# A hybrid SSD and attention layer on one core: another order of issue for its middle part

## The chip, the cores and the metric

The kernel runs on one core of a Trainium2 chip. The metric is the device time of one execution in microseconds, lower is better; the kernel before is given by the median of three runs, beside the lowest and the highest. The engines of the core are TensorE (PE in the profile, with PEld for its weight loads), VectorE (DVE), ScalarE (ACT), GpSimd (POOL) and SyncE (SP, which here only issues transfers).

## The reference

One layer of a trunk with two groups of heads in parallel, Mamba-2 SSD heads and latent attention (MLA) heads, and a SwiGLU FFN, for 512 columns of a new stream (prompt) and 64 columns of a running one (sample). All in fp32.

```python
def hybrid_layer(x, ckv_past, krope_past, ssm_h0, conv_buf, p):
    h = rmsnorm(x, p['norm_mix'])
    proj = h @ p['w_in']                      # z, xbc, dt, cq, ckv
    ...
    xbc, conv_new = causal_conv(xbc, conv_buf, p['conv_w'], p['conv_b'])
    ...
    y, h_new = ssd_scan(xh, dt, A, Bm, Cm, ssm_h0)        # chunks of 64
    y = y + p['d_skip'].astype(jnp.float32)[:, None] * xh.astype(jnp.float32)
    y = y.reshape(b, T, SSD_WIDTH) * jax.nn.silu(z.astype(jnp.float32))
    y_ssd = rmsnorm(y, p['ssd_norm']).astype(x.dtype)
    ...
    o_lat = mla_attend(q_lat, q_rope, q_pos, keys_c, keys_r, jnp.arange(P + T))
    o = jnp.einsum('bthl,lhd->bthd', o_lat, p['w_uv']).reshape(b, T, MLA_WIDTH)
    x = x + jnp.concatenate([y_ssd, o], axis=-1) @ p['w_out']
    hf = rmsnorm(x, p['norm_ffn'])
    x = x + (jax.nn.silu(hf @ p['w_gate']) * (hf @ p['w_up'])) @ p['w_down']
    return x, c_kv, k_rope, h_new, conv_new
```

The model width is 1024, the FFN's 2816; 8 SSD heads and 8 attention heads of 64; the sample stream has 256 past positions. Outputs are the normed x of both groups, the new latent and rotary keys, the SSD states and the convolution's last rows.

## The kernel before

**Tiling.** The 576 columns (512 prompt and 64 sample) are cut into two halves of 288, which are the free size of the large products; features lie in tiles of 128 on the partitions. An fp32 product is made of three: weights and operand are each split into a high part (ScalarE copies it to fp32r, L120) and a low part (VectorE subtracts, L121 for weights, L154 in `split_scaled` for operands), and `product` issues high·high, high·low and low·high for each 128 of the contraction. So a tile named `wl_...` is the low part of a weight, and a product needs both.

**Stages.** 1. The first tiles of the input projection. 2. Convolution tiles (`conv_tile`, L396), with small copies of the tiles' ends to `nconv` on POOL (L405, L406). 3. The SSD scan, chunk by chunk, with the z tiles (`z_tile`, L471), the v tiles (L602) and the projections of head pairs (`pair_proj`, L618) between. The cumulated steps are transposed on TensorE, copied by VectorE to `cumT` (L386) and written to DRAM as `cumD` by POOL (L387, in `step_rows`); `chunk_a` loads rows of it back on SP as `cumb` (L496) and `ecp` (L502), POOL masks `cumb` with an affine_select (L523, `chunk_e`), and ScalarE makes the decays E of it (L529). 4. Attention by pairs of heads: `scores` (L673) into PSUM tiles `sc` (prompt blocks, two heads) and `sc_s` (sample); `soft` (L656) takes the negated maximum on VectorE (`mx`, L663), the exponential with its sum on ScalarE (`pr`, L664), the reciprocal (`sm`, L665) and the scaling (L670); `turn` and `turn_s` (L692, L706) transpose `pr` on TensorE into `ptp` and copy it to `pt`; `values` makes `pv` and `pvs`, and `cat` (L715) splits them into the operand `cat_o`: ScalarE's copies (L719), then VectorE's subtractions (L720). 5. Output projection: `cat_tile` (L771) makes the operands `cat_y` of the SSD heads (xsd L772, then the low part `a`, L154), and `out_tile` (L746) multiplies: tiles `ps_o0_t` take the SSD heads (weights `wl_out0`, `wh_out0`), tiles `ps_o1_t` the attention heads; VectorE adds each half of a tile into x (L758), which frees its PSUM bank. 6. `x_operands` (L809) makes the FFN's operands `xop` and `xop_last` (seven blocks of a Strassen-like scheme with seven products), with subtractions of `x` blocks (L824 to L827) and low parts (L831); `gu_weights` (L834) makes the combined weights (additions L840 to L843, then `split_weights`). 7. The FFN, from about 240 us to the end: gate and up products (L883), down products, the last norm and the outputs.

**PSUM.** Most tiles of stages 3 to 5 come from a pool `bank(tag, name)` (L455) with three banks under "sc", and banks under "pp" and "hm": a new tile waits until the reader of an earlier one in the same bank is done.

**Order.** All instructions are first made stage by stage. Then `issue_in_order` (L1327) chains the instructions of each engine in the order of a table `ISSUE` (L1339): a text of places among those made on that engine, which `_places` decodes ("469-634" stands for a run). Each engine then issues strictly in this order, and its instructions wait for their operands by semaphores. The table covers 4190 places on TensorE, 893 on VectorE, 688 on ScalarE, 160 on POOL and 133 on SP. SP's list is the order of the loads, each of which is issued only when the one before it could be.

```python
for name, text in ISSUE.items():
    made = [i for i in nc.cur_bb.bb.instructions if i.engine == engines[name].engine]
    order = list(_places(text))
    for a, b in zip(order, order[1:]):
        tc.add_manual_dep(made[b], made[a].name, info, reason="issue order")
```

Of the kernel before, what the change touches and what calls it, by code (L numbers as in the profile page):

```python
# [1326 lines left out]
def issue_in_order(tc, nc):  # L1327
# [15 lines left out]
154-169 174-175 170-171 270-274 176-221 172-173 222-269 275-370 373-420 371 421-468 372 469-634 637 641-644 638-640  # L1343
657-660 635-636 665-726 737-758 661-664 763 645-652 759-760 727-736 764-766 653-656 767-818 859 761-762 819-826 860-864
833-840 827-832 865-870 841-852 871-874 853-856 875-880 857-858 881-887 904-912 888 892-899 889-891 900-903 925-926
913-921 927-934 922-924 935 939-940 936-938 949-957 964-966 941 945-948 967-968 958-963 969 942-944 970-975 987 976-979
1003 980-986 991-993 988 1004-1005 1015-1021 1006-1014 1022-1024 994-996 1025-1026 1029-1034 1043-1045 997-998 989
1000-1002 999 1046-1054 990 1035-1039 1059-1061 1040-1042 1062-1064 1027-1028 1075-1077 1081-1092 1055-1057 1078-1080
1093-1096 1058 1097-1104 1121-1123 1071-1072 1124-1129 1065 1068-1070 1073 1105-1107 1066-1067 1074 1130-1156 1119-1120
1229-1240 1157 1108-1114 1158 1241-1245 1253-1262 1246-1247 1115-1118 1159-1161 1176-1177 1248-1252 1263-1264 1162-1175  # L1350
1265 1180 1178 1181-1183 1179 1266-1268 1277-1279 1184-1187 1190-1195 1269-1276 1196-1204 1188-1189 1205-1223 1227-1228
1224-1226 1280-1297 1301-1303 1298-1300 1304-1321 1342-1343 1348-1355 1344-1347 1322-1341 1356-1511 1572 1512-1559
1575-1576 1560-1571 1577 1596-1598 1578 1573-1574 1593 1584-1585 1579 1581-1583 1602-1604 1623-1625 1594-1595 1614 1586
1605-1606 1590-1592 1611-1613 1632-1634 1587-1589 1608-1610 1607 1580 1599-1601 1620-1622 1641 1626-1628 1647-1649
# [10 lines left out]
81 57 65 56 89 66 83 90 130 91 95 84 96-97 46 98-100 113-114 103 115 47 139 116 93 117 92 111 118 122-123 148 124  # L1365
101-102 125 120 126-127 119 131-133 155 134 129 135-136 140-142 149 104 152 128 150 153 170 143-144 138 145 147 151 154
156 137 146 174 157 178 159 171-172 187 169 160 158 161-162 176 203 163 175 183 180 164 167 165-166 168 211 181 177 188
173 189 182 184 190-191 179 192-194 185-186 220 195 204-206 196-202 207 282 208 212-214 209 216 218 215 210 221 217 219
222-225 228 226-227 229-230 239 249 240 231 288 250 241 233 242 251 253 252 254 234 232 258 235 255 236 257 256 301 261
237 259 238 260 243 262 264 245 263 247 244 268 246 248 269-270 283 265 284 271-273 289 280 274 276 275 281 266 291 311  # L1370
285 277 312 267 292 296 293 310 294 278-279 313 297 300 286-287 290 303 306 298 320 299 304 302 307 321 356 305 322 316
295 317 308 357 324 318 314 323 309 330 315 319 358 327 361 331 325-326 359 334 332 328-329 335 338 343 333 344 339 336
340 346 345 337 349 352 360 341 353 351 342 354 350 347 355 362 371 348 364-365 363 366 369-370 367-368 376 384 372 378
377 379-380 373 383 381 374 391 382 375 387 399 389 385 390 388 386 394 393 395 392 397 396 414 400 398 402 401 403 406
404 411 408 405 407 412 456 410 415 417 413 458 419 416 418 409 427 425 420 426 423 422 421 432 424 428 463 457 430 429
431 433 436 435 437 460 434 438 445 459 440 461-462 446-447 439 441 449 448 442 467 469 450 471 470 468 451 466 464 472
452-453 443-444 473 454 475 474 455 465 476 485 481 477 490-491 478 482 492-493 483 494-496 479-480 497 504 484 509-512
516 486 498 513 500 514 501 515 502 526-529 533 540 487-489 530 541-543 499 505-506 503 517 531 523-524 518-519 507-508
525 532 534 522 544 535 560 520 536 521 545 537 539 546 538 561-562 547-548 563 549 568 564 550-553 555 569-570 554 559
571 556 572-575 565 576-577 566 557 584-585 578 586 579-580 558 592 567 593-594 587-588 581-582 595 583 597 596 589  # L1380
598-601 590 604 591 602-603 614-617 605 621 606 618 607-608 619-620 613 628-630 622 631 611 632 612 623 610 609 624 635
633 625 634 627 626 648-650 636 651 637 656 652 638-641 643 657-658 642 647 659 644 660-663 653 664-665 654 645 672-673
666 674 667-668 646 680 655 681-682 675-676 669-670 683 671 685 684 677 686-689 678 692 679 690-691 702-705 693 709 694
706 695-696 707-708 701 716-718 710 719 699 720 700 711 698 697 712 723 721 713 722 715 714 736-738 724 739 725 744 740
726-729 731 745-746 730 735 747 732 748-751 741 752-753 742 733 760-761 754 762 755-756 734 768 743 769-770 763-764
757-758 771 759 773 772 765 774-777 766 780 767 778-779 790-793 781 797 782 794 783-784 795-796 789 804-806 798 807 787
808 788 799 786 785 800 811 809 801 810 803 802 824-826 812 827 813 833 828 814-817 819 834-835 818 823 836 820 837-840
829 841-842 830 821 849-850 843 851 844-845 822 858 831 859-860 852 832 853 846-847 861 848 863 862 854 864-867 855 870
856 868 874 869 875-877 881 878 857 879 871 880 873 872 882-892
# [3 lines left out]
64 44 46-48 53-54 68 55 57-58 72 59 61-62 76 63 65-67 77 69-71 73 92 74-75 94 79 88 78 81 104 82 90 84 116 86-87 103 85  # L1393
83 100 98 80 97 89 99 102 101 96 91 126 105 93 111 109-110 156 115 95 107-108 113 122 114 112 142 117 163 106 118-119
136 127 137 134 128 140 135 124 121 120 139 129 138 141 130 123 143 131 125 150 146 149 132 210 133 145 148 154 152 151
# [127 lines left out]
```

## Time and profile before

| | before |
|---|---|
| median of 3 runs | 629.37 us (628.84 to 630.38) |
| the profiled execution's own time | 629.94 us |
| its span in the profile | 628.2 us |
| granted clock, mean | 0.997 |
| TensorE, VectorE, ScalarE, POOL busy | 99%, 86%, 64%, 19% of the span |
| DMA | 89.19 MB, mean 142 GB/s |

A row of a timeline gives the start, the duration, the engine, the line of the kernel, and the operation as output <- inputs, where the engine's idle time ahead of it and what ended it stand in brackets. Matmuls are pipelined: one of 288 columns shows some 0.29 us, though the next starts 0.13 us later. A chain of waits is read from the end backwards: each piece is what released the next. The number of instructions in a row (x3) follows the tiles' names, which stand without their buffer numbers.

### The profile page before, as it was taken

How to read it: one execution, taken by the hardware profiler on the slowest of the kernel's cores; microseconds unless marked ns; L12 is line 12 of the kernel's file. 1: busy time of each engine (PE TensorE's matmuls, PEld its weight loads, DVE VectorE, ACT ScalarE, POOL GpSimd, SP SyncE). 2: the span in 40 equal slices, each digit the busy share in tenths (PEclk: the TensorE clock that was granted, in tenths of full speed). 3: DMA queues.
4: the chain of work that ended last, by engine and by line, in shares of the span. 5: the costliest groups of instructions: out<-in, count | busy, mean ns of one | idle time of the engine just before them, and what ended most of it. 6: DMA issues, size and time to landing. Idle time of an engine off the chain costs nothing.

```text
span 628.2 us, 12100 instructions
## 1 busy us (share of the span) xinstructions
PE 618.9 (99%) x4639; PEld 592.2 (94%) x4639; DVE 539.6 (86%) x941; ACT 399.6 (64%) x767; POOL 117.1 (19%) x169
## 2 busy tenths in 40 slices
PE   9999999999999999999999999999999999999996
PEld 8899999986788799999999999999999999999996
DVE  6999986889876699999999888988899789986556
ACT  7655445779775577766566676666757664767364
POOL 1322104231010000001300330033104220313322
PEclk9999999999999999999999999999999999999998
DMA  8322374322241123235633986398737893589924
GB/s 318 139 62 73 93 197 130 116 75 76 79 141 39 59 111 105 84 122 182 246 142 106 202 185 150 98 186 192 181 101 154 200 213 100 97 217 261 251 46 150
DMA packets 39593, 89.19 MB, mean 142 GB/s; under 512 B 4570, under 2 KB 14312, under 8 KB 39280
## 3 DMA queue, kind: packets, MB, share of 16 engines
q1 hardware_dynamic: 26416, 63.12, 30.5%
q0 software_dynamic: 12400, 24.73, 21.3%
q8 instruction: 36, 0.59, 0.4%
q10 hardware_dynamic: 720, 0.57, 0.3%
q14 instruction: 21, 0.17, 0.1%
HBM read 62.74 MB, written 24.53 MB: 139 GB/s over the span
## 4 chain that ended last, share of the span: by engine, by line
PE 89%; DVE 7%; issue 1%; ACT 1%; DMA 1%; POOL 0%; POOLq 0%; DVEq 0%; ACTq 0%
PE ps_x L883 21%; PE ps_d L1073 14%; PE ps_z L883 10%; PE ps_in L289 7%; PE ps_y L883 5%; PE ps_z L466 4%; PE ps_o L466 4%; PE ps_first L138 3%; PE ps_l L289 3%; PE ps_d L289 2%; PE sc L680 2%; PE ps_p L883 2%; PE pv L727 1%; PE ptp L702 1%; PE ps_q L466 1%
## 5 line engine op out<-in xcount | busy, mean ns | idle before, releaser
L883 PE MATMUL ps_x<-xop,wh_gu_S 128*128 128x288 f32 x378 | 75.9, 292 | 0.0
L121 DVE TENSOR_TENSOR wl_gu_S<-gu,wh_gu_S 128x1024 fp32r<-128x1024 f32 x44 | 53.3, 1220 | 8.3 <-ACT wh_gu_S L120 6.0
L883 PEld LDWEIGHTS ps_x<-xop,wh_gu_S 128*128 128x128 f32 x378 | 60.1, 188 | 0.2 <-ACT u L986 0.2
L1087 POOL DMA_DIRECT2D acc<-fz x32 | 27.9, 906 | 164.3 <-ACT fz L1084 135.7
L120 ACT CAST wh_gu_S<-gu 128x1024 fp32r<-128x1024 f32 x44 | 46.3, 1052 | 15.3 <-PE ps_y L883 7.8
L883 PE MATMUL ps_x<-xop,wl_gu_S 128*128 128x288 f32 x189 | 55.1, 291 | 0.0
L883 PEld LDWEIGHTS ps_x<-xop,wl_gu_S 128*128 128x128 f32 x189 | 35.4, 188 | 0.0
L120 ACT CAST wh_gu_A<-gu 128x1024 fp32r<-128x1024 f32 x22 | 23.1, 1049 | 10.4 <-PE ps_x L883 7.1
L883 PE MATMUL ps_z<-xop,gu_a 128*128 128x288 f32 x189 | 29.3, 291 | 0.0
L466 PE MATMUL ps_o<-a,wh_out 128*128 128x288 f32 x128 | 28.6, 308 | 0.4 <-DVE a L154 0.3
L121 DVE TENSOR_TENSOR wl_gu_A<-gu,wh_gu_A 128x1024 fp32r<-128x1024 f32 x22 | 26.8, 1220 | 1.2 <-ACT wh_gu_A L120 0.7
L1032 POOL DMA_DIRECT2D acc<-dn x8 | 4.4, 544 | 120.3 <-ACT dn L1031 120.3
L289 PE MATMUL ps_in<-a,wh_in 128*128 128x288 f32 x128 | 26.1, 296 | 0.5 <-DVE sp_a L369 0.5
L883 PE MATMUL ps_x<-xop_last,wh_gu_S 128*128 128x288 f32 x126 | 26.5, 291 | 0.0
L883 PEld LDWEIGHTS ps_z<-xop,gu_a 128*128 128x128 f32 x189 | 26.3, 187 | 0.0
L1073 PE MATMUL ps_d<-pair,d_1h 128*128 128x288 f32 x128 | 26.1, 292 | 0.0
L883 PE MATMUL ps_z<-xop,wh_gu_S 128*128 128x288 f32 x126 | 25.8, 293 | 0.0
L289 PE MATMUL ps_in<-xs,wh_in 128*128 128x288 f32 x128 | 25.7, 293 | 0.0
L466 PE MATMUL ps_o<-cat_o,wh_out 128*128 128x288 f32 x128 | 25.4, 293 | 0.2 <-DVE x L758 0.2
L883 PE MATMUL ps_x<-xop,wh_gu_A 128*128 128x288 f32 x126 | 25.5, 293 | 0.0
L883 PE MATMUL ps_y<-xop,wh_gu_A 128*128 128x288 f32 x126 | 25.5, 293 | 0.0
L289 PE MATMUL ps_l<-pr,wh_dl 128*128 128x320 f32 (+1 forms) x128 | 25.4, 294 | 0.0
(434 smaller groups left out, 2216.7 us busy)
## 6 DMA issues: line engine op xcount, KB each, us to landing
gu<-in_w_gu SPq DMA_DIRECT2D x44, 512.0 KB, 5.3
wr_d<-in_w_down SPq DMA_DIRECT2D x18, 512.0 KB, 3.8
acc<-fz POOLq DMA_DIRECT2D x16, 288.0 KB, 7.1
acc<-da POOLq DMA_DIRECT2D x16, 288.0 KB, 8.0
acc<-dc POOLq DMA_DIRECT2D x16, 288.0 KB, 8.6
wr_in<-in_w_in SPq DMA_DIRECT2D x8, 512.0 KB, 3.8
wr_out<-in_w_out SPq DMA_DIRECT2D x8, 512.0 KB, 3.3
cumb<-cumD SPq DMA_DIRECT2D x5, 512.0 KB, 4.5
```

Of the source, the lines that this page charges most:

```text
L120: act.copy(hi, raw)
L121: dve.tensor_tensor(lo, raw, hi.bitcast(F32), ALU.subtract)
L138: pe.matmul(ps[:m, hf, : cols.stop - cols.start], w, x[:, cols], start=start and k == 0 and i == 0, stop=stop and k == last and i == 2,)
L289: pe.matmul(ps, w, x[:, cols], start=first and k == 0 and i == 0, stop=last and k == len(terms) - 1 and i == 2,)
L466: pe.matmul(ps[:, :n], w, x[:, cols], start=k == 0 and i == 0, stop=k == len(terms) - 1 and i == 2,)
L680: pe.matmul(s[:, :nk], qs[:, j, q0 : q0 + P], ks[:, j, :nk], start=True, stop=True)
L702: pe.transpose(pp[:, k : k + P], prs[p, i][:, j, b * P : b * P + P], ident)
L727: pe.matmul(pv[64 * j : 64 * j + 64, b * P :], V[b][:, h * HD : (h + 1) * HD], pts[p, b, j], start=b == 0, stop=True, skip_group_check=b > 0,)
L883: pe.matmul(ps, p, q, start=not onto and first and kp == kps[0] and j == 0, stop=onto or (last and kp == kps[-1] and j == 2), skip_group_c ...
L1032: pool.dma_start(acc[1][t], dn)
L1073: pe.matmul(ps, p, v, start=not onto and n == 0 and j == 0, stop=onto or (n == len(ks) - 1 and j == 2), skip_group_check=onto,)
L1087: pool.dma_start(out, src, accum_op=ALU.add)
```

## The change

The lists of places in `ISSUE` are replaced. The instructions are the same ones: on each engine the new list is a permutation of the old. In which part it differs:

| engine | places that differ | time of that part before | instructions moved | furthest move |
|---|---|---|---|---|
| TensorE | 600 to 1494 | 88.9 to 238.7 us | 660 | 68 places |
| VectorE | 111 to 460 | 68 to 269 us | 249 | 22 |
| ScalarE | 91 to 339 | 103 to 273 us | 174 | 21 |
| POOL | 31 to 80 | 72.9 to 304 us | 42 | 13 |
| SP | 45 to 59 | 101 to 135 us | 10 | 2 |

On TensorE the halves of z tiles and of output tiles, which stood one after the other, are interleaved with each other and with transposes and score products; runs of transposes are cut into smaller ones (places "1105 1141-1144 1106 1145-1149" and the like). The transposes ptp0_0 go ahead of the scores sc1_3_1; one ps_y of chunk 1 is split by a product of a v tile. On POOL the write of cumD (30) goes behind the nconv copies of four later tiles (34 to 42), and the affine_selects go ahead of several issues of qs. On VectorE the additions that make cat_o1 (328 and 329) go ahead of wl_out0_7 (361) and of an addition of ps_o (358); at the FFN's start an addition of gu (457) goes from before the writes of xop_last (433, 435) to behind the last of them. On SP some ecp loads, wr_uv, wr_pair1 and an output change places with a neighbour.

```diff
     "PE": """
...
-154-169 174-175 170-171 270-274 176-221 172-173 222-269 275-370 373-420 371 421-468 372 469-634 637 641-644 638-640
-657-660 635-636 665-726 737-758 661-664 763 645-652 759-760 727-736 764-766 653-656 767-818 859 761-762 819-826 860-864
...
+154-169 174-175 170-171 270-274 176-221 172-173 222-269 275-370 373-420 371 421-468 372 469-599 613-614 600-606 615-621
+607-612 622-624 637 625-626 638 627-632 665-674 633-634 641-642 639-640 643-644 635 675 636 657 676-680 689-690 658 691
...
     "DVE": """
...
-295 317 308 357 324 318 314 323 309 330 315 319 358 327 361 331 325-326 359 334 332 328-329 335 338 343 333 344 339 336
...
+320-321 304 299 316 356 322 317 295 357 307 323 308 324 314 309 359 318 330 325 319 315 327 326 331 328-329 332 305 358
+333 361 335 334 338 343 360 336 344-345 337 339-340 346 349 352 347 353 341 348 342 351 354 350 355 371 364 363 362
...
     "POOL": """
-0-3 7 18 28 4 8 5 9 6 10 26 11 27 12 29 13-17 20-23 19 24-25 31 30 32-42 57 59 61 63 58 60 62 64 43-48 52-54 49-51 55-56
...
+0-3 7 18 28 4 8 5 9 6 10 26 11 27 12 29 13-17 20-23 19 24-25 31 34-35 37 32-33 40 42 39 41 30 38 36 57 43-44 61 59 45-48
+52-53 60 63 58 54 49-51 55 62 64 56 65-66 70 69 67-68 74 71-73 75 77 79 76 81 83 85 87 80 82 78 89 84 86 88 90-93 95 94
...
     "SP": """
-11-14 16 15 17-20 23 22 25 21 24 31 26 32 39-40 36 33 38 41-42 37 43-47 55 77 62 79 54 56 58 63 81 57 60 59 61 68 66 72
-67 65 76 69-71 78 73 86 64 74-75 87 80 88-89 84 90 85 91 98 101 99-100 102-103 106-165
+11-14 16 15 17-20 23 22 25 21 24 31 26 32 39-40 36 33 38 41-42 37 43-47 55 77 62 79 54 56 58 63 81 57 60 59 61 68 67 66
+72 65 76 69 78 73 70-71 86 75 64 74 87 80 88-89 84 90 85 91 98 101 99-100 102-103 106-165
```

More of the change, by code (lines that the diff above doesn't have):

```diff
@@ new lines @@
+853-854 875 880 855-856 842 876 843 877-879 857 881 884 904 885-886 858 910 905-906 911 844 882-883 887 907 888-889 908
+892-899 909 890-891 912 900-903 913-919 925-926 920-921 927-935 922-924 939-940 936-938 949 952-953 950-951 954-957
+964-966 941 945-948 967 958 968 959-963 969 942-944 970-974 976-979 975 1003 987 980 984 981-982 985 991-993 1004 988
+1005 1015 1006 1016-1017 983 986 1007 1018-1019 1008-1010 1020-1021 1011-1014 1022-1026 994 1029-1034 995-996 1043-1045
+989 997 1000-1001 998-999 1046-1048 1002 1049-1054 990 1035-1038 1059-1060 1027-1028 1061-1062 1039-1041 1063 1042 1064
@@ new lines @@
+1572 1512-1559 1575-1576 1560-1571 1577 1596-1598 1578 1573-1574 1593 1584-1585 1579 1581-1583 1602-1604 1623-1625
+1594-1595 1614 1586 1605-1606 1590-1592 1611-1613 1632-1634 1587-1589 1608-1610 1607 1580 1599-1601 1620-1622 1641
+1626-1628 1647-1649 1642-1643 1615-1616 1635-1637 1617-1619 1638-1640 1653 1656 1658-1667 1644-1646 1629-1631 1650-1652
+1654-1655 1668-1669 1657 1682 1694-1705 1683-1693 1670-1681 1730-1741 1706-1729 1742-1748 1754-1755 1749-1753 1756-1767
+1778-1785 1768-1777 1786-1885 1898-1905 1886-1897 1906-2017 2030-2036 2018-2029 2037-2053 2066-2084 2054-2065 2085-2089
@@ L1361 @@
+2102-2104 2090-2101 2105-2221 2234-2236 2240-2241 2222-2233 2237 2242-2248 2238-2239 2249-2725 2738-2740 2744 2726-2737
+2741 2745-2751 2742-2743 2752-3229 3242-3244 3248 3230-3241 3245 3249-3255 3246-3247 3256-3733 3746-3748 3752 3734-3745
+3749 3753-3759 3750-3751 3760-4189
 """,
@@ L1389 @@
[L1389 removed]
+81 57 65 56 89 66 83 90 130 91 95 84 96-97 46 98-100 113-114 103 115 139 116 93 92 117-118 122 102 123 148 124 120 101
+125-126 47 127 131-132 129 133 119 155 134-135 111 136 140-141 104 142 149 152 170 150 143-144 153 145 154 156 128 147
+138 151 137 174 157 159 158 171 146 172 187 160-162 169 176 175 163 178 173 177 203 164-165 180-181 183 188 166-167 189
+182 168 190-193 179 184 194 211 185 220 186 195 204 196 205 197 206 200 198-199 201-202 282 207 212 208 213 218 214 209
@@ new lines @@
+692 679 690-691 702-705 693 709 694 706 695-696 707-708 701 716-718 710 719 699 720 700 711 698 697 712 723 721 713 722
+715 714 736-738 724 739 725 744 740 726-729 731 745-746 730 735 747 732 748-751 741 752-753 742 733 760-761 754 762
+755-756 734 768 743 769-770 763-764 757-758 771 759 773 772 765 774-777 766 780 767 778-779 790-793 781 797 782 794
+783-784 795-796 789 804-806 798 807 787 808 788 799 786 785 800 811 809 801 810 803 802 824-826 812 827 813 833 828
+814-817 819 834-835 818 823 836 820 837-840 829 841-842 830 821 849-850 843 851 844-845 822 858 831 859-860 852 832 853
@@ new lines @@
+499-500 509-510 503 518-519 505-507 504 508 511 520 512 521 514-515 513 516-517 522 530-531 523 532 524 528 525 529 527
+526 533 538 534 539-540 536 535 537 541 549 542 550 543 548 545 547 544 557 546 558 551 566-567 553-556 559 568 561 569
+562-563 560 564-565 552 570 575 572 576 571 573-574 583-584 577 592-593 579-581 578 582 585 594 586 595 588-589 587
+590-591 596 604-605 597 606 598 602 599 603 601 600 607 612 608 613-614 610 609 611 615 623 616 624 617 622 619 621 618
+632 620 633 625 641-642 628-631 634 643 636 644 637-638 635 639-640 626 645 650 627 651 647-648 646 649 659-660 652
```

105 lines of the change are left out of this document (44 added, 61 removed).

## The prediction

> **What bounds the kernel now.** I read the page first, then busy time by stretches of the part whose order changes, then TensorE's waits, and last the chain inside the one stretch where TensorE waits at all.
>
> ```profile
> PE 618.9 (99%) x4639; PEld 592.2 (94%) x4639; DVE 539.6 (86%) x941; ACT 399.6 (64%) x767; POOL 117.1 (19%) x169
> ```
> ```profile
> PE 89%; DVE 7%; issue 1%; ACT 1%; DMA 1%; POOL 0%; POOLq 0%; DVEq 0%; ACTq 0%
> ```
>
> TensorE (PE) is busy for 618.9 us, 99% of the span, and 89% of the chain that ended last runs through it. The diff only permutes places in the lists; no instruction is added or dropped. So the change can gain what TensorE waits in its stretch and what its order costs in pace, and it can lose by new waits.
>
> On TensorE the first 600 places are the same, up to about 89 us, and the last place that differs lies at about 239 us; on VectorE (DVE) the places differ from 68 to 269 us and on ScalarE (ACT) from 103 to 273 us. So I asked for the busy time by stretches (columns: PE, weight loads, DVE, ACT, POOL, then clock and DMA):
>
> ```profile
> 100.00:145.00 45.00, 45.00 (x357) 41.05 (x356) 35.13 (x68) 33.33 (x89) 11.27 (x10) 1.00 0.30 96
> 145.00:152.00 7.00, 6.80 (x37) 4.96 (x35) 6.80 (x17) 6.90 (x22) 0.00 (x0) 1.00 0.10 28
> 152.00:160.00 8.00, 6.82 (x32) 3.94 (x33) 7.98 (x21) 7.62 (x21) 2.00 (x4) 1.00 0.67 226
> 160.00:170.00 10.00, 9.65 (x65) 7.59 (x63) 8.09 (x18) 6.93 (x17) 0.00 (x0) 1.00 0.02 6
> 170.00:240.00 70.00, 70.00 (x528) 60.35 (x529) 53.07 (x118) 44.85 (x107) 2.02 (x4) 1.00 0.27 90
> 240.00:275.00 35.00, 34.78 (x259) 33.88 (x258) 34.93 (x67) 24.46 (x43) 0.00 (x0) 1.00 0.26 87
> ```
>
> TensorE waits 0.20 + 1.18 + 0.35 us between 145 and 170 and 0.22 us between 240 and 275: 1.95 us in all. In the other 115 us it never waits. The granted clock is 1.00 throughout, so the clock plays no part. The waits by what ended them:
>
> ```profile
> PE sc L680 <- ACT pr L664: 1.1, 2, 0.9
> PE ps_o L466 <- DVE a L154: 0.3, 1, 0.3
> PE sc_s L686 <- ACT pr L664: 0.2, 1, 0.2
> PE ps_o L466 <- DVE x L758: 0.2, 1, 0.2
> ```
>
> The first three lie at 152 to 160.7. There VectorE is busy 7.98 of 8 us, and the chain shows who is behind ScalarE's part (start, us, what):
>
> ```profile
> 146.72 1.02 DVE mx L663 x2
> ...
> 159.22 0.73 DVE xsd L772
> 159.95 0.68 DVE a L154
> 160.63 0.04 issue
> 160.67 2.26 PE ps_o L466 x15
> ```
>
> From 146.72 to 160.63 the chain runs through VectorE alone: maxima of the scores, the scaling of the probabilities, the norm of y, and then xsd (L772) and the low part `a` (L154) of the cat_y tiles. TensorE resumes for good at 160.67, when the second cat_y tile's low part is there. That stretch is bound by VectorE; all the rest of the changed part is bound by TensorE.
>
> **The change part by part.** All terms are made against the profiled execution's own 629.94 us (1.7 us more than its span). It stands 0.57 us above the median of 629.37; I carry the sum over to the median.
>
> (A) Before 145 us, one move is large: the write of cumD (POOL, L387) goes behind the nconv copies of four later conv tiles.
>
> ```profile
> 72.92 0.54 POOL L387 DMA_DIRECT2D cumD<-cumT  x1 [8.07 <-DVE cumT L386]
> ...
> 85.22 0.19 POOL L406 COPY nconv<-up 128x3 f32<-128x3 f32 x1
> 94.68 3.85 POOL L624 DMA_DIRECT2D qs<-rrp  x8 [9.26 <-DVE rrp L445]
> 98.53 0.71 POOL L523 TENSOR_SCALAR_AFFINE_SELECT cumb<-cumb 64x512 f32<-64x512 f32 x1
> ```
> ```profile
> 84.18 0.44 SPq L496 DMA_DIRECT2D cumb<-cumD  x1
> ```
> ```profile
> cumb<-cumD SPq DMA_DIRECT2D x2, 512.0 KB, 6.3
> ...
> cumD<-cumT POOLq DMA_DIRECT2D x1, 20.0 KB, 1.6
> ```
>
> It was issued at 72.92; now it cannot be issued before the copies at 85.2 are done, so at 85.4, and it lands 1.6 us later, at about 87. SP's load of cumb (chunk 4) went out at 84.18 and must now wait for it, some 3 us, with the ecp loads and the weights wr_z1 queued behind it on SP. It lands at about 87 + 0.4 + 6.3 = 93.7. What hides this: the affine_select on that cumb ran only at 98.53, because it stood behind eight qs issues on POOL (94.68 + 3.85 = 98.53), and the new order puts it before most of those eight. So the mask comes no later than before, perhaps 3 us earlier, and nothing gains, since TensorE did not wait there. The cover is 98.5 − 93.7, nearly 5 us. The qs issues themselves go to about 110 to 130 us; their first readers, the scores, come just ahead of the maxima at 146.72. Term: 0; bounds 0 and, with the cover gone, rival 3.
>
> (B) 145 to 160.7. The set of VectorE instructions ahead of the one that releases TensorE at 160.67 is the same in both lists (268 instructions), and so is the set ahead of the first of them that waits for the last SSD state; in between, neighbours change places by at most five. A sum does not depend on its order, and VectorE has no hole there to fill. The transposes of pr_0_0 now stand ahead of scores sc1_3_1 and wait for them to be scaled, but that wait runs into the same gate at 160.67. Term −0.1; bounds −0.2 (VectorE's idle in 145 to 152 gone) and 0.
>
> (C) Finer mixing. Over the changed stretch TensorE changes from 288-column projection products to the 128-column transposes or scores and back 50 times before and 107 times after: 57 more round trips. The price of one:
>
> ```profile
> 162.51 0.29 PE L466 MATMUL ps_o<-a,wl_out 128*128 128x288 f32 x1
> 162.64 0.29 PE L466 MATMUL ps_o<-a,wh_out 128*128 128x288 f32 x1
> 162.77 0.49 PE L702 MATMUL ptp<-ident,pr 128*128 128x128 f32 x3
> 163.02 0.38 PE L466 MATMUL ps_o<-a,wh_out 128*128 128x288 f32 x1
> 163.23 0.29 PE L466 MATMUL ps_o<-a,wl_out 128*128 128x288 f32 x1
> 163.37 0.42 PE L466 MATMUL ps_q<-cqn,wh_pair 128*128 128x288 f32 x2
> ```
> ```profile
> 131.98 0.33 PE ps_x L506 x3
> ```
>
> Products follow each other at 0.13 us (162.51 to 162.64) and transposes at 0.11 (0.33 for three). From 162.64 to 163.37 stand three products and three transposes, by these paces 0.39 + 0.33 = 0.72 us; the trace has 0.73. One round trip costs about 0.01 us. With rounding it is between 0.004 and 0.016: 57 of them cost 0.2 to 0.9 us. I take 0.008 each, +0.45.
>
> [...]
>
> (D) Half-array runs.
>
> ```profile
> 134.54 1.02 PE ps_y L550 x16
> 135.57 0.86 PE ps_g L595 x6
> ```
>
> The 64-wide ps_y takes 16 instructions in pairs side by side: eight passes at 0.11 are 0.88, and the chain has 1.02; the six ps_g behind it should take 0.66 and take 0.86. One visit so costs between 0 and 0.34 us. There are 13 visits before and 14 after (one ps_y is split by a v tile). Term +0.2; bounds 0 and +0.35.
>
> (E) 160 to 240. No wait is there to remove, so only new ones count. The nearest candidate: on VectorE both additions of cat_o1 (L720), which need ScalarE's copies, move five places up.
>
> ```profile
> 196.17 1.22 DVE L121 TENSOR_TENSOR wl_out<-wr_out,wh_out 128x1024 fp32r<-128x1024 f32 x1
> 197.30 0.69 DVE L663 TENSOR_REDUCE mx<-sc 128x1 f32<-128x512 f32 x1
> ...
> 200.36 0.67 DVE L720 TENSOR_TENSOR cat_o<-pv,cat_o 128x512 fp32r<-128x512 f32 x1
> ```
> ```profile
> 198.68 0.21 ACT L719 CAST cat_o<-pvs 128x64 fp32r<-128x64 f32 x1
> ```
>
> Before, they ran at 200.36, well after the copies, the last of which ends at 198.89. Now VectorE comes to them when the maximum of 197.30 is done, and that is about 1.2 us earlier, as wl_out0_7 is no longer ahead of it: at about 196.8. There it stands some 2 us. Behind it are queued, in this order, the scaling of pr_2_4, an addition of ps_o into x (L758), and wl_out0_7 with its 1.22 us; the next addition of ps_o comes to about 204.5 by adding up these durations, where TensorE's next half tile that wants the bank comes at about 204.0. So 0.5 us of a wait for one bank. Such halves of ps_o0 and ps_o1 tiles are interleaved with transposes in several places, so a second is possible; and TensorE may come later too, when it waited elsewhere. Term +0.4; bounds 0 and +1.0.
>
> (F) The first FFN tiles, 240 to 264. TensorE's order is the same from place 1512 on; VectorE's is not. It is saturated (34.93 of 35 us).
>
> ```profile
> 254.59 0.69 DVE L841 TENSOR_TENSOR gu<-gu,gu 128x512 f32<-128x512 f32 x1
> ...
> 262.48 2.35 DVE L121 TENSOR_TENSOR wl_gu_S<-gu,wh_gu_S 128x1024 fp32r<-128x1024 f32 x2
> ```
> ```profile
> 265.41 0.29 PE L883 MATMUL ps_z<-xop,wl_gu_S 128*128 128x288 f32 x1
> ```
>
> The addition of gu that ran at 254.59 (L841) and a half write of xop_last go behind other writes of xop_last (L831), which so come about 0.69 us earlier, and wl_gu_A11 too; the 0.22 us that TensorE waits here, and pauses of a few tenths at 257 and 260 that the trace counts as busy, can shrink. Against it, that addition now stands ahead of the two wl_gu_S of 262.48: the second ends at about 262.48 + 2.35 + 0.69 = 265.5, and TensorE wanted it at 265.41, a new 0.1. Term −0.3; bounds −1.0 and +0.1.
>
> Sum: 0 − 0.1 + 0.45 + 0.2 + 0.4 − 0.3 = **+0.65 us**: 630.6 against the profiled 629.94, and 630.0 against the median. All low ends together give −1.0 (628.4), all high ends +2.35 (631.7).
>
> **The rivals.** A difference of about 0.3%, 1.9 us, is what a measurement of this kernel can tell from no change.
>
> Rival 1, faster: the new order takes away the waits at 152 to 160.7 and at the FFN's start without making others. That is at least the 1.95 us idle: 629.37 − 1.95 = 627.4. For it: the largest wait (0.9 us) is for ScalarE's exponentials, and their order did change. Against it: they need VectorE's maxima, VectorE has no hole there, and (B) shows its work ahead of the gate unchanged. Chance 0.13.
>
> Rival 2, slower: VectorE's stand at cat_o1 makes not one late bank but several. The order is fixed, so its hole of 198.89 − 196.8 = 2.1 us cannot be used by what stands behind, and each late addition of ps_o (L758) passes its lag on to the half tile that wants the bank. At the first such place 0.5 us of it reaches TensorE by (E); if the whole 2.1 us does over several banks, the time is 629.37 + 0.65 − 0.4 + 2.1 = 631.7. It decides from the point where an addition of ps_o ends after TensorE stands at the next half tile. Against it: 17 us of idle VectorE in 170 to 240 (70.00 − 53.07) in which it catches up. Chance 0.14.
>
> [...]
>
> Rival 3, slower: the late cumD holds SP's queue, and with it wr_z1 and the other chunks' rows, so long that the SSD chunks start late. It decides from about 5 us more than I worked out in (A); then each further us is a us of TensorE's wait, say 2: 629.37 + 0.65 + 2 = 632.0. Against it: the write has only POOL copies of 0.2 us ahead, which follow additions that TensorE's unchanged first 600 places release. Chance 0.06.
>
> That the change does nothing, because the places moved lie in slack, is inside the forecast (629.4).
>
> **How the numbers follow.** Forecast with its bounds 0.67 (628.4 to 631.7), Rival 1 0.13, Rival 2 0.14, Rival 3 0.06. Predicted is the forecast, 630.0. The range goes from 627.8 to 631.7: it holds the forecast whole and half of Rival 2, and leaves out most of Rival 1 and Rival 3. Faster by over 0.3% (below 627.5): most of Rival 1, 0.12. Slower by over 0.3% (above 631.26): Rivals 2 and 3, mostly, and the upper end of the forecast, 0.21. Within: 0.67.
>
> **What would show it.** (A): the affine_select on chunk 4's cumb no later than 98.5, and no TensorE wait before 145. (B): TensorE's wait for `a` (L154) ends at 160.5 to 160.7 and the waits for pr (L664) stay within 0.3 us in sum. (C) and (D): 170 to 240 longer by 0.3 to 1 us at full busy time. (E): a wait of ps_o for x (L758), or for wl_out, near 204. (F): fewer waits at 248 to 264, one at 265.4. I am wrong if VectorE's release at 160.67 comes more than 0.5 us earlier, or if TensorE shows waits of over 1 us anywhere between 160 and 240.

## The result, and the profile after

The changed kernel is **slower**: 633.95 us in the median of five runs (632.58 to 635.33), against 629.87 us of the kernel before beside it; the ratio is 1.0065 [1.0044, 1.0085], some 4.1 us. The prediction of 630.0 us is too low, and its range, which ends at 631.7, does not hold the time. The profiled execution took 632.80 us with a span of 631.1, 2.9 us more span than before.

The page of the changed kernel, its busy line and the chain by engines:

```profile
PE 620.6 (98%) x4639; PEld 592.6 (94%) x4639; DVE 538.2 (85%) x941; ACT 400.1 (63%) x767; POOL 119.0 (19%) x169
```
```profile
PE 70%; DVE 10%; issue 3%; ACT 3%; DMA 1%; POOL 0%; SPq 0%; POOLq 0%; DVEq 0%; ACTq 0%
```

Every engine has its old number of instructions. TensorE is busy 1.7 us longer in a span 2.9 us longer. The shares of the chain need care: here it can be followed back only to 79.7 us, so 13% of the span is missing, where that of before went back to 0.8 us. In what is left, VectorE, ScalarE and issue together have 7 points more than before: somewhere the chain leaves TensorE. Busy time by stretches of the changed kernel, with one stretch more at the start than the prediction showed:

```profile
88.00:100.00 12.00, 10.99 (x80) 9.79 (x79) 10.43 (x17) 3.77 (x9) 3.03 (x4) 1.00 0.80 226
100.00:145.00 45.00, 45.00 (x355) 40.46 (x353) 33.55 (x68) 31.77 (x84) 14.78 (x15) 1.00 0.31 95
145.00:152.00 7.00, 7.00 (x37) 5.45 (x37) 6.87 (x16) 5.88 (x17) 0.00 (x0) 1.00 0.17 54
152.00:160.00 8.00, 6.28 (x31) 3.27 (x30) 7.92 (x23) 7.91 (x24) 1.98 (x4) 1.00 0.48 158
160.00:170.00 10.00, 9.83 (x68) 8.50 (x68) 8.49 (x16) 6.87 (x18) 0.00 (x0) 1.00 0.18 69
170.00:240.00 70.00, 69.87 (x515) 59.33 (x512) 50.98 (x118) 44.48 (x106) 1.91 (x4) 1.00 0.24 80
240.00:275.00 35.00, 34.93 (x260) 34.01 (x259) 34.91 (x67) 25.52 (x44) 0.00 (x0) 1.00 0.33 106
```
```profile
88.00:100.00 12.00, 12.00 (x93) 11.49 (x93) 10.88 (x18) 3.35 (x7) 4.56 (x9) 1.00 0.86 218
```

The second fence is the same view of the kernel before. Between 88 and 100 us TensorE now waits 1.01 us where it waited for nothing, and starts 80 matmuls instead of 93. The other stretches show almost no wait more than before. So the windows find about 1 us of the 2.9.

**A better ruler.** TensorE's old and new list both have 4190 places, so I compare when it starts its N-th: start of place N in a run less start of place N in the profile of before. Where that difference grows between two places, TensorE lost time there, whether or not the trace calls it busy. (The order within a stretch differs, so the ends lie where both orders have done nearly the same work. Some products, ps_y among them, leave two records in the trace for one place.) In us, for profiled executions:

| kernel | 622-759 (92-110 us) | 759-946 (-144) | 946-1061 (-171) | 1061-1501 (-240) | 1501-1685 (-265) |
|---|---|---|---|---|---|
| changed | +1.77 | +0.87 | −0.59 | +2.00 | −0.45 |
| changed, a second time | +5.79 | +0.91 | +1.51 | +2.01 | −0.45 |
| before, a second time | 0 | 0 | 0 | 0 | 0 |

With the −0.71 us by which the changed run was ahead at place 622 (a start-up difference at 5 to 7 us, which the second run of before has too, −0.82), the first row adds up to the 2.9 us of span. It has **two losses that the windows hide**: 0.87 us where TensorE shows 45.00 busy of 45, and 2.00 us where it shows 69.87 of 70.

### The profile page after: what moved, and what is told of

Read it like the earlier page. It is cut to its first block, busy times and chain, and to the rows that moved or that the text cites. A ratio compares the mean times of both kernels' runs of the same rounds, so it can differ in the third digit from the quotient of the medians.

```text
span 631.1 us, 12104 instructions
## 1 busy us (share of the span) xinstructions
PE 620.6 (98%) x4639; PEld 592.6 (94%) x4639; DVE 538.2 (85%) x941; ACT 400.1 (63%) x767; POOL 119.0 (19%) x169
## 4 chain that ended last, share of the span: by engine, by line
PE 70%; DVE 10%; issue 3%; ACT 3%; DMA 1%; POOL 0%; SPq 0%; POOLq 0%; DVEq 0%; ACTq 0%
PE ps_x L883 21%; PE ps_d L1073 14%; PE ps_z L883 10%; PE ps_y L883 5%; PE ps_o L466 3%; PE ps_z L466 3%; PE ps_d L289 2%; PE ps_l L289 2%; PE sc L680 1%; PE ptp L702 1%; PE pv L727 1%; DVE x L758 1%; DMA wr_z<-in_w_in 1%; DVE xop L831 1%; PE ps_v L613 1%
## 5 line engine op out<-in xcount | busy, mean ns | idle before, releaser
L466 PE MATMUL ps_o<-a,wh_out 128*128 128x288 f32 x128 | 30.9, 318 | 0.2 <-DVE a L154 0.2
```

Of the source, the lines that this page charges most:

```text
L466: pe.matmul(ps[:, :n], w, x[:, cols], start=k == 0 and i == 0, stop=k == len(terms) - 1 and i == 2,)
```

## The experiments

Three theories: the late write of cumD delays a load of weights that the z tiles need; the finer mixing on TensorE and its neighbours' order make small pauses; TensorE's clock drops after the thinner stretch at 152 to 160 us. All kernels hold the same instructions; only `ISSUE` differs. Ratios are to the kernel before in the same session, whose medians were 629.48 to 630.22.

**The two halves.** `first_part` has the new lists up to TensorE's place 946, VectorE's 227, ScalarE's 168, POOL's 65 and SP's 60, and the old ones from there; `second_part` the reverse.

```diff
# second_part, to before ("PE", from place 946 on)
-964-966 941 945-948 967-968 958-963 969 942-944 970-975 987 976-979
...
+964-966 941 945-948 967 958 968 959-963 969 942-944 970-974 976-979 975 1003 987
...
```

> The changed lists up to about 143 us, and the lists of before from there on. If the parts add: +1.8 at 89 to 126 and +0.6 at 126 to 142, so 2 to 2.6 us slower than before. Rival (the VectorE-bound stretch at 145 to 160 takes a late start up): within 1 us of before.

> The kernel before up to about 143 us on all five engines, and the changed lists from there on. From the ladder of lags in the profile: -0.4 at 145 to 170, +2.0 at 170 to 240, -0.4 at the FFN's start, so 1.0 to 1.5 us slower than before if the parts add. Rival (what is lost after 143 follows only from the late start of the first part): within 0.4 us of before.

Measured: `first_part` 632.90 us, 1.0044 [1.0024, 1.0065], `second_part` 631.45 us, 1.0028 [1.0013, 1.0043]: +2.8 and +1.35, together 4.15, the 4.1 of the whole. By places `first_part` loses 2.02 and 0.91 and then nothing; `second_part` −0.45, +1.97, −0.45. The halves add up, so each can be studied alone; two thirds lie before 145 us, where (A) is 0 and only shares of (C) and (D) stand.

**The write of cumD.** The chain of waits of the changed kernel, 84.9 to 98.8 us (start, us, what):

```profile
84.93 2.77 DMA cumD<-cumT
...
87.72 0.33 SPq L496
...
88.09 0.66 SPq L502
...
88.80 6.66 DMA wr_z<-in_w_in
...
95.53 1.05 ACT wh_z L120
...
96.61 1.23 DVE wl_z L121
97.84 0.38 DVE zh L476
...
98.26 0.54 PE ps_z L466 x2
```

cumD was written 12 us later than before, 84.93 instead of 72.92. SP holds cumb (L496) and ecp (L502) until it has landed, at 87.70, and only then issues the weights wr_z1 that stand behind them: at 88.80, against 86.99 in before. They land at 95.46; before they landed at 92.91. ScalarE makes wh_z1 of them and VectorE wl_z1, and behind wl_z1 in VectorE's queue stands zh (L476), which empties the z bank that TensorE wants. The issue of wr_z1 by SP in before:

```profile
86.99 0.33 SPq L127 DMA_DIRECT2D wr_z<-in_w_in  x1
```

VectorE's timeline of the changed kernel shows the place where the load reaches the z bank (idle time before and its cause in brackets):

```profile
96.61 1.23 DVE L121 TENSOR_TENSOR wl_z<-wr_z,wh_z 128x1024 fp32r<-128x1024 f32 x1 [0.99 <-ACT wh_z L120]
97.75 0.45 DVE L476 SCALAR_TENSOR_TENSOR zh<-ps_z,R 128x288 f32<-128x288 f32 x1
```

The last product that zh reads starts at 96.80, so zh could have run some 0.6 us earlier; it stands behind wl_z1. In before the same zh started at 97.67, hardly sooner. The difference is on TensorE, which in the old order comes back to that bank at place 673 (98.77 us in before) and in the new one at place 662. `cum_back` is the changed kernel with POOL's and VectorE's old places for cumD; `cum_late` is the kernel before with the new ones.

```diff
# cum_back, to after (POOL, VectorE)
-31 34-35 37 32-33 40 42 39 41 30 38 36 57 43-44
+31 30 32-42 57 43-44
-117-118 122 102
+117-118 111 122 102
...
-134-135 111 136
+134-136
# cum_late, to before
-31 30 32-42
+31 34-35 37 32-33 40 42 39 41 30 38 36
-92 111 118
+92 118
...
-135-136
+135 111 136
```

> The changed kernel with one thing undone: the write of cumD stands again ahead of the nconv copies on POOL, and VectorE's copy cumT early on VectorE; all other lists as changed. Theory Q (SP's queue behind the late cumD is what costs at 88 to 100 us): wr_z1 lands again at about 92 to 93 instead of 95.5, TensorE's waits at 91.9 to 98.3 go, and of the 1.8 us lost between places 600 and 853 at least 1.4 come back: 1.4 to 2 us faster than the changed kernel. Theory M (the mixed order of z tiles itself, with halves that wait for VectorE's zh and half-array transposes cut apart): only the last of the waits, 0.4 us at 98.3, goes; 0.3 to 0.7 us faster than the changed kernel.

> The kernel before with this alone: the write of cumD goes behind the nconv copies of four later tiles on POOL, and cumT late on VectorE. Theory Q: SP's loads behind it go out 2 to 3 us later, wl_z1 and with it the zh behind it on VectorE come about 2 us later, and TensorE, which needs that bank at 98.8, waits: 1 to 2 us slower than before. Rival (the cover named in the prediction holds): within 0.3 us of before.

Measured: `cum_back` 633.16 us, 1.0048 [1.0030, 1.0066]; `cum_late` 630.96 us, 1.0015 [1.0001, 1.0030]. Neither the whole loss taken away nor the whole made: the late write in the old order costs 0.9 us (0.1 to 1.9 by the interval), and its return gives the changed kernel about 1, with intervals that overlap. Because the size varied, I ran the changed kernel and `cum_back` again side by side, as `changed_again` and `cum_back_again`.

> The changed kernel itself once more, beside cum_back_again on the same chip. The loss between places 622 and 759 was 1.8 us in one profile of these lists, 2.0 in a second and 0.3 in a third (att_back), so it should vary from execution to execution with the landing of wr_z1: if wr_z1 lands before 94.5 us (counted from the same start), the loss is under 0.8 us, else 1.3 or more. Time 3.5 to 5 us above before.

> The changed kernel with the write of cumD and VectorE's cumT early again, once more, beside changed_again on the same chip. Theory Q: 0.8 to 1.5 us faster than changed_again in the medians, and 0.7 us or less lost between places 622 and 759. Rival (the mixing alone costs there): within 0.4 us of changed_again.

Measured: 635.18 us (632.21 to 640.19), 1.0087 [1.0053, 1.0120], and 632.67 us (631.76 to 634.05), 1.0043 [1.0028, 1.0058]. Side by side the early write saves **2.5 of 5.0 us**, with intervals that still touch. Both sessions together give 11 executions with the late write, in the median 4.3 us over the kernel before, and 12 with the early one, 2.6 us over it: the write's share is some 1.6 us. In both profiles with the early write the wait at 98.3 us is gone, and the one near 93.6 stays, as the second theory of `cum_back` said; but `cum_back_again` lost 1.33 us at 622-759, where 0.7 or less was expected. What TensorE lost there, from the profiled executions, split at place 640 (VectorE's stand for wl_z2 is explained below; the last two columns are what is lost beyond the 0.32 us of `att_back`, whose TensorE waits for nothing here):

| kernel | TensorE's order there | cumD | VectorE stood for wl_z2, us | wr_z1 landed, us | lost, us | up to place 640 | from there on |
|---|---|---|---|---|---|---|---|
| before | old | early | 0 | 92.91 | 0 | | |
| cum_late | old | late | 0 | 95.43 | 0.27 | | |
| cum_back_again | new | early | 1.26 | 91.71 | 1.33 | 1.18 | −0.17 |
| cum_back | new | early | 0.79 | 92.99 | 0.67 | 0.52 | −0.17 |
| att_back (below) | new | late | 0 | 93.95 | 0.32 | 0 | 0 |
| changed | new | late | 1.06 | 95.46 | 1.77 | 1.00 | 0.45 |
| first_part | new | late | 0.30 | 95.56 | 2.02 | 0.24 | 1.46 |
| changed_again | new | late | 0 | 97.45 | 5.79 | 0 | 5.47 |

From place 640 on the loss goes with wr_z1, and so with cumD: nothing is lost there with weights by 94.0, and 0.45, 1.46 and 5.47 us with weights at 95.46, 95.56 and 97.45. In the old order the weights may come at 95.43 and cost 0.27 us, because TensorE comes back to that z bank later.

**A second load.** Ahead of place 640 stands something else, and in the changed profile it takes more than the write of cumD: 1.00 of the 1.77 us. VectorE's new list puts wl_z2 (170) three places earlier, ahead of qt0 (150) and qt1 (153), and two of the cacc ahead of qt1. VectorE at wl_z2, before and after, and what TensorE waits for then:

```profile
89.06 1.22 DVE L121 TENSOR_TENSOR wl_z<-wr_z,wh_z 128x1024 fp32r<-128x1024 f32 x1
```
```profile
87.57 1.23 DVE L121 TENSOR_TENSOR wl_z<-wr_z,wh_z 128x1024 fp32r<-128x1024 f32 x1 [1.06 <-ACT wh_z L120]
```
```profile
91.86 0.27 PE L506 MATMUL ps_x<-ident,xsd 128*64 128x128 f32 x1 [0.27 <-DVE qt L444]
93.63 0.50 PE L466 MATMUL ps_z<-a,wh_z 128*128 128x288 f32 x2 [0.33 <-DVE zh L476]
```

The weights wr_z2 landed at 86.41, no later than in before (86.99); but now VectorE is there first and stands for them, and qt1 and the first zh, which are behind wl_z2 on VectorE, come late. The stand and the loss up to place 640 go together in all six profiles of the table with the new order, and in `zh_ahead`, `mid_back` and `four_back` below (0.73 and 0.67, 0.66 and 0.60, 1.07 and 0.89). No run puts wl_z2 back alone, so this cause rests on the traces.

The worst execution, `changed_again`, in its chain, TensorE's timeline, and by stretches:

```profile
89.28 8.17 DMA wr_z<-in_w_in
...
98.60 1.23 DVE wl_z L121
99.83 0.38 DVE zh L476
```
```profile
100.25 0.85 PE L466 MATMUL ps_z<-a,wh_z 128*128 128x288 f32 x2 [2.69 <-DVE zh L476]
```
```profile
100.00:110.00 10.00, 9.75 (x54) 9.69 (x55) 4.66 (x8) 5.56 (x15) 2.38 (x4) 0.69 0.46 115
```

The same 512 KB took 8.17 us instead of 6.66. TensorE then waited 2.69 us, and behind that wait its granted clock was 0.69 in the mean of 100 to 110 us. By estimate that clock cost 0.31 × 10 = 3.1 us; with the wait that is the 5.79 us lost by the ruler, so the wait was paid about twice.

A try to cure the place, `zh_ahead`, which puts one of VectorE's zh ahead of wl_z1:

```diff
# zh_ahead, to after (VectorE)
-151 137 174 157 159 158
+151 137 157 174 159 158
```

> The changed kernel with one VectorE instruction moved: zh (157), the evacuation that frees a z bank, goes ahead of wl_z1 (174). Theory Q2 (the late cumD reaches TensorE through two queues in order: SP holds wr_z1, and on VectorE zh stands behind wl_z1, which needs it): without touching cumD, TensorE's wait of 0.4 us at 98.3 goes, places 622 to 759 lose 1.3 instead of 1.8 us, 0.4 to 0.6 us faster than the changed kernel. Rival (wl_z1 itself is what TensorE needs next, so the wait only moves on to it): no gain between 622 and 759.

Measured: 636.04 us, 1.0094 [1.0071, 1.0116], no cure. In its profile wr_z1 landed at 97.47, as late as in `changed_again`. The wait of 2.69 us for zh is gone, and 622-759 lost 1.93, of which 0.67 up to place 640; but the next stretch lost 2.61, since xdt stands behind wl_z1 too. TensorE's waits of that run have this successor:

```profile
PE ps_x L506 <- DVE xdt L508: 1.1, 1, 1.1
```

`z_mix` puts TensorE's new places 600 to 853 alone into the kernel before:

```diff
# z_mix, to before ("PE")
-469-634 637 641-644 638-640
+469-599 613-614 600-606 615-621
...
```

> The kernel before with TensorE's changed list only between places 600 and 853 (z tiles by halves, transposes cut apart), the write of cumD early as before. Theory Q (the late cumD costs most there): 0.5 to 0.8 us lost between places 600 and 853, as in the kernel that had cumD moved back. Theory M (the mixing costs most): 1.2 us or more.

Measured: 636.86 us, 1.0115 [1.0096, 1.0134], dearer than the whole change. Two of TensorE's waits in it:

```profile
PE ps_g L595 <- ACT ysq L592: 2.2, 1, 2.2
PE ps_z L466 <- DVE zh L476: 2.0, 1, 2.0
```

The new TensorE order needs the new orders of ScalarE and VectorE beside it; a piece of it alone does not price the mixing. `mid_back`, the changed kernel with the old lists for 123 to 144 us, missed in the same way.

```diff
# mid_back, to after ("PE", places 853 to 946; the others' alike)
-871 845-848 872-873 849-852 874 853-854 875 880 855-856 842 876 843
+839-852 871-874 853-856 875-880 857-858 881-887
...
```

> The changed kernel with the lists of before put back at 123 to 143 us on all engines. If the loss of that part (0.8 us between places 853 and 946) is its own: that loss goes to 0, 0.8 us faster than the changed kernel. Rival (the late start of the first part makes it): 0.5 us or more of it stays.

Measured: 646.44 us, 1.0255 [1.0238, 1.0273], with one wait of 5.3 us of ps_g for ScalarE's ysq (L592). So what makes the 0.9 us at 759-946 is not separated; it is 0.85 to 0.92 us in six profiles with the new lists there and ahead of it (`zh_ahead` apart), whether TensorE comes to it early or late.

**From 171 to 240 us.** Here TensorE's timeline must be read by starts, not by busy time: products follow each other at 0.13 us. `second_part`:

```profile
171.46 0.42 PE L466 MATMUL ps_o<-a,wh_out 128*128 128x288 f32 x2
171.96 0.40 PE L466 MATMUL ps_o<-a,wl_out 128*128 128x288 f32 x1
172.19 0.42 PE L466 MATMUL ps_o<-a,wh_out 128*128 128x288 f32 x2
```
```profile
170.69 1.21 DVE L121 TENSOR_TENSOR wl_out<-wr_out,wh_out 128x1024 fp32r<-128x1024 f32 x1
177.32 0.46 DVE L630 COPY qs<-ps_q 64x288 f32<-64x288 f32 x1
```

Two products from 171.46 should be over at 171.72; the next starts at 171.96, just after VectorE's wl_out0_2 (170.69 + 1.21 = 171.90). That is a wait of 0.24 us, and the list of waits has none: a record of 0.29 us for a pace of 0.13 covers 0.16 us of a pause, and the 0.08 us left, from 171.88 to 171.96, are not listed. A second stands at 177.8, behind the copy of qs1. `vector_early` moves these two forward on VectorE:

```diff
# vector_early, to second_part (VectorE)
-273 291 266 274 277 311 276
+273 291 311 266 274 277 276
-293 275 297 310 287
+293 310 275 297 287
```

> The kernel with the changed lists only from 143 us on, and in it two VectorE instructions moved up: wl_out0_2 (311) by three places, the evacuation of ps_q into qs1 (310) by two. Theory V (the pauses at 172 to 178 are TensorE waiting for these two, which the changed VectorE list brings late): between places 1061 and 1096 TensorE loses about 0.1 us against before instead of 0.67, and the time is 0.5 to 0.6 us less than without the two moves, about 630.9. Theory P (the finer mixing on TensorE itself costs pace): that loss stays at 0.6 or more.

Measured: 630.37 us, 1.0011 [0.9999, 1.0022], against 1.0028 [1.0013, 1.0043] in another session. The loss in 1061-1501 goes from 1.97 to 1.40, that in the first part of it (1061-1096) from 0.67 to 0.02. TensorE's starts at the same place:

```profile
171.51 0.42 PE L466 MATMUL ps_o<-a,wh_out 128*128 128x288 f32 x2
171.77 0.29 PE L466 MATMUL ps_o<-a,wl_out 128*128 128x288 f32 x1
171.90 0.42 PE L466 MATMUL ps_o<-a,wh_out 128*128 128x288 f32 x2
```

171.77 − 171.51 is 0.26 for two, the pace. So 0.6 of the 2.0 us are late VectorE results. The other 1.4 are lost between 188 and 240 us in many pauses of at most 0.4 us; whether they are late results too or the price of the finer mixing was not tried.

`cat_back` undoes what the prediction feared most, VectorE's early additions of cat_o1:

```diff
# cat_back, to second_part (VectorE)
-331 328-329 332 305 358 333 361 335
+331-332 305 358 333 361 328-329 335
```

> The kernel with the changed lists only from 143 us on, with the two additions of cat_o1 (328, 329) put back behind wl_out0_7 (361) on VectorE. Step E of the prediction (VectorE's stand at cat_o1 makes the additions of ps_o late): between places 1200 and 1361 TensorE loses 0.4 to 0.5 us less than without the move. Rival (TensorE has no wait from it): that loss stays within 0.1 us of 0.49.

Measured: 631.92 us, 1.0038 [1.0023, 1.0052], no gain; places 1200 to 1361, around cat_o1, lose 0.54 us with it and 0.49 without. Yet VectorE does stand there, in the changed kernel's timeline:

```profile
201.21 0.69 DVE L720 TENSOR_TENSOR cat_o<-pv,cat_o 128x512 fp32r<-128x512 f32 x1 [1.95 <-ACT cat_o L719]
```

1.95 us of idle VectorE cost TensorE nothing. `others_second` takes the new lists of VectorE, ScalarE and POOL in this part, with TensorE's old one:

```diff
# others_second, to before: VectorE 276-402, ScalarE 209-296, POOL 71-75 new
-285 277 312 267 292 296 293 310 294 278-279
+276 285 267 278 312 292 279 286 290 293 275
...
```

> The kernel before with the changed lists of VectorE, ScalarE and POOL only between about 165 and 240 us; TensorE's list is that of before. Theory V: the late VectorE results cost as much without the mixing on TensorE, 1 us or more lost between places 1061 and 1501. Theory P: less than 0.3 us lost. If both lists only fit each other, the loss can be above 2 us.

Measured: 634.85 us, 1.0080 [1.0066, 1.0093]; 1061-1501 lost 5.38. The new lists of the other engines fit only the new one of TensorE. The converse, TensorE's new list there alone, wasn't tried.

**The clock.** `kept_parts` keeps only what the ruler shows as gains (TensorE 946-1061 with its neighbours, and VectorE's and ScalarE's FFN start); `att_only` keeps only the first of these; `att_back` is the changed kernel without it.

```diff
# att_only, to before ("PE" 946-1061; VectorE 227-276, ScalarE 169-209, POOL 67-71; att_back: the reverse, to after)
-964-966 941 945-948 967-968 958-963 969 942-944 970-975 987 976-979
+964-966 941 945-948 967 958 968 959-963 969 942-944 970-974 976-979 975
...
# kept_parts: att_only, and the new VectorE 403-460 and ScalarE 296-339
```

> The kernel before with the changed lists only where the ladder shows gains: all engines at 143 to 166 us, and VectorE and ScalarE at the FFN's start from 240 us on. If the gains are of these places alone: -0.45 at each, 0.9 us faster than before, about 629.2. Rival (the gain at the FFN's start only takes back what was lost right before it): -0.45 us, or none.

> The kernel before with the changed lists only at 143 to 166 us. Theory C: a dip of the granted clock to 0.5 somewhere in 150 to 166 us is likely (one in two), and the median is 0 to 0.7 us above that of before, with more spread. Rival: 0.3 to 0.5 us faster than before, clock 1.00.

> The changed kernel with the lists of before put back at 143 to 166 us on all engines. The changed lists there bring TensorE 0.4 us forward in the ladder, but its waits closer together: its least busy 3.4 us have 1.95 us of work instead of 2.26. Theory C (the granted clock halves for some 3 to 7 us after these waits in about half of the executions of the changed lists, at 1 to 2.4 us each): put back, the profile shows the clock at 1.00 through 150 to 166 us, and the median falls by about 0.5 us in spite of the 0.4 us lost. Rival (the dips are chance, as common in both orders): 0.4 us slower than the changed kernel.

> The kernel before itself, for one more profile. Theory C: the clock stays at 1.00 between 150 and 166 us. Rival: it dips here as often.

Measured: `kept_parts` 629.37 us, 1.0000 [0.9989, 1.0011]; `att_only` 629.72 us, 0.9995 [0.9985, 1.0005]; `att_back` 635.03 us, 1.0072 [1.0046, 1.0099]; `old_again`, the kernel before in one execution, 629.64 with no drop of the clock near 155 us. A thin stretch of 3.4 us near 155, in before, after and `att_only`, and what followed in the last:

```profile
151.00:154.40 3.40, 2.26 (x11) 0.93 (x11) 3.34 (x12) 3.36 (x14) 1.30 (x3) 1.00 0.07 15
```
```profile
154.00:157.40 3.40, 1.95 (x8) 0.56 (x9) 3.37 (x12) 3.40 (x12) 1.98 (x4) 1.00 0.26 59
```
```profile
152.00:155.40 3.40, 2.02 (x7) 0.98 (x6) 3.40 (x11) 3.40 (x12) 1.98 (x4) 0.84 0.39 86
155.00:158.40 3.40, 3.40 (x9) 2.07 (x9) 3.40 (x8) 3.32 (x8) 0.00 (x0) 0.50 1.03 396
158.00:161.00 3.00, 3.00 (x12) 2.33 (x11) 3.00 (x5) 1.71 (x3) 0.00 (x0) 0.50 0.51 174
```

With the new lists TensorE is busy 1.95 and 2.02 of 3.4 us in these windows, with the old ones 2.26. (In `att_only` the drop begins inside the window, whose mean clock is 0.84; the one from 151.0 to 154.4 us has 2.11 of 3.4 at 0.99.) In 7 of 12 profiles with the new lists the granted clock then fell to 0.50 for 3.4 or 6.8 us, at a cost of 0.95 to 2.46 us; in 7 profiles with the old lists, never at this place. The same lists ran with a drop and without one: `changed_again` had 0.50 at 161 to 165 us, and the first profile of the changed kernel 1.00 from 140 to 170 us. What decides it in an execution is not shown. The medians deny the clock a part in the 4.1 us: `att_only` is as fast as before, and `att_back`, without the new lists there, is no faster than the changed kernel. A wider spread is not shown either: the 12 executions of `att_only` took 628.89 to 631.65 us, 17 of before beside it 629.16 to 631.92.

The kernel of `att_only`, run once more as `att_only_2`, took 678.97 us at a mean granted clock of 0.85 and tells nothing on this. `four_back` put four undone pieces together:

```diff
# four_back, to after: the edits of cum_back, vector_early, mid_back and cat_back
```

> The changed kernel with all of these put back or moved together: cumD and cumT early, the lists of before at 123 to 143 us, wl_out0_2 and the evacuation of ps_q up on VectorE, and cat_o1 behind wl_out0_7. If the parts add: 1.1 + 0.8 + 0.65 and 0 to 0.5 us less than the changed kernel, so 1 to 1.5 us slower than before. If the mixed lists lose as much elsewhere once these are gone: 2 us or more slower than before.

Measured: 645.69 us, 1.0246 [1.0230, 1.0262]: `mid_back`'s misfit again. No version beat the kernel before clear of the noise.

## Why the prediction was wrong

**(A) failed, in two steps.** The first is the wait on SP's queue. (A) priced the late cumD at nothing because the affine_select on chunk 4's cumb (L523) had nearly 5 us of cover. That much held: POOL reaches it at 96.77 in the changed kernel, ahead of the 98.53 of before. But SP's queue was followed only to the mask. The text itself names "the weights wr_z1 queued behind it on SP" and then asks nothing of them; they came 2.55 us later, and through wh_z1, wl_z1 and zh stopped TensorE: for 0.45 us in this profile, 1.46 and 5.47 in two others with the late write, and not in a fourth. Rival 3 named this queue and this load, with a chance of 0.06 and "from about 5 us more" as the point of decision: that point belonged to the mask. wr_z1 had no such cover in the new order of TensorE, where the z bank is wanted sooner. In the medians the early write gives back some 1.6 us.

The second is VectorE. "One move is large", says (A), and looks at none of VectorE's moves before 145 us; wl_z2 moved by three places only, and VectorE's stand for it cost TensorE 1.00 us of this profile and 0 to 1.18 of others. Term 0; measured at 622-759 1.8 and 2.0 us in two profiles and 5.8 in a third.

The waits of the changed kernel, behind 88 us:

```profile
PE sc L680 <- ACT pr L664: 0.8, 1, 0.8
PE ps_z L466 <- DVE zh L476: 0.7, 2, 0.4
PE ptp L702 <- DVE pr L670: 0.7, 1, 0.7
PE ps_x L506 <- DVE qt L444: 0.3, 1, 0.3
PE sc_s L686 <- ACT pr L664: 0.2, 1, 0.2
```

Those of ps_z and ps_x lie at 91.6 to 98.3 us and are new: the one of ps_x and one of ps_z come behind wl_z2, the other of ps_z behind wl_z1.

**(B) held in its mechanism.** VectorE still bounds the stretch: the waits for pr are 0.8 + 0.7 + 0.2 = 1.7 us, against 1.3 before, a little more than the 0.3 allowed. TensorE's wait for `a` ends in the chain at

```profile
161.71 0.68 DVE a L154
...
162.44 0.66 PE ps_o L466 x3
```

162.44; less the 1.93 us by which TensorE was already late (−0.71 + 1.77 + 0.87) that is 160.51, within the 160.5 to 160.7 given. Both orders stand at place 999 then, so the release gained 0.16 us, where (B) had 0.1. The whole stretch gained 0.45 to 0.59; where the rest comes from is open, and in some executions the clock takes it back (`changed_again` lost 1.51 us at 946-1061, with 0.50 at 161 to 165 us).

**(C) held in size, at most.** `second_part`'s TensorE, at a new visit of one transpose:

```profile
183.41 0.43 PE L466 MATMUL ps_o<-a,wh_out 128*128 128x288 f32 x2
183.67 0.27 PE L702 MATMUL ptp<-ident,pr 128*128 128x128 f32 x1
183.70 0.38 PE L466 MATMUL ps_o<-a,wl_out 128*128 128x288 f32 x1
183.91 0.42 PE L466 MATMUL ps_o<-a,wh_out 128*128 128x288 f32 x2
```

From 183.41 to 183.91 are three products and a transpose: 0.39 + 0.11 = 0.50 us, and the trace has 0.50. Four such visits between places 1121 and 1142 cost 0.01 us or less each. So 57 cost 0 to 0.5 us, which does not make what was lost. (Counted in the lists, TensorE leaves the z, output and head-pair products 27 times before and 79 times after, so 52 times more and not 57; that changes the term by 0.04.) Whether it is the 0.008 taken or nothing, 0.01 us of rounding does not decide.

**(D)** can't be sized. Its "16 instructions" of ps_y are eight in the kernel (L550), with two records each. Its stretch, 759-946, lost 0.9 us at full busy time; half-array runs and late results are not separated.

**(E) had the right place for VectorE's stand and the wrong victim.** The 1.95 us at cat_o1 came as worked out (2 us) and cost TensorE nothing; Rival 2 falls with it. Of the 2.0 us of 171 to 240, 0.6 are other late results, wl_out0_2 and qs1; the rest is not assigned. The prediction's opening sentence of (E), "No wait is there to remove, so only new ones count", rests on 70.00 busy of 70.00, a number that cannot show pauses of tenths. In the changed kernel busy time misleads too, 69.87 of 70.00 beside 2.0 us lost: the records look longer than their share, 0.29 us at a pace of 0.13.

**(F)** gained 0.45, near its −0.3, but only right behind a loss: alone, in `kept_parts`, the same lists give 0.04. So it seems to take back what was just lost, and does not shorten the part by itself; the prediction asked which order is shorter, not what happens when TensorE arrives late.

In sum +0.65 was predicted; the profile has 1.77 + 0.87 − 0.59 + 2.00 − 0.45 = +3.6 on the same terms. The misses are the +1.8 at 622-759, where (A) has 0 (in this profile 1.00 behind wl_z2, 0.45 behind wr_z1 and 0.32 without a listed wait), and the 2.9 of 759-946 and 1061-1501, where (C) to (E) have 1.05.

## What to carry to other kernels

When a DMA moves later, follow each load queued behind its reader on the same queue to the engine that waits for it, not only the reader itself; "hidden" must be said of every one of them. Look at small moves too: an instruction that needs a load, moved forward in an engine's fixed order, makes all behind it wait for that load (VectorE stood 1.06 us for wl_z2, three places earlier, and qt1 and zh came late). Compare two orders by the start times of the N-th matmul: TensorE showed as busy for 69.87 of 70 us through pauses that added up to 2.0. The engines' orders fit each other: part of the new ones alone cost 5.4 us (`others_second`) and 7.4 (`z_mix`) over the kernel before, so undo matching stretches on all engines, and see first that the halves add up.

## What the runs showed of the hardware

The granted clock fell to 0.50 behind a stretch in which TensorE was still busy 2.11 of 3.4 us (`att_only`, 151.0 to 154.4), without a full stop, and stayed at 1.00 behind one of 1.95 of 3.4 (the first profile of the changed kernel). Such a drop came in 7 of 12 profiles with the new lists, and in none of the 7 with the old lists there (2.26 of 3.4 in before). The 512 KB load of wr_z1 took 6.66 us in one execution and 8.17 in another of the same kernel, and with its landing 2 us later what TensorE lost behind it went from 0.45 to 5.47 us: a wait of 2.69 us, and behind it a granted clock of 0.69 in the mean of 100 to 110 us.
